# Experts of a two-layer trunk: weights as the stationary operand in plain fp32, sorted by token count

## Chip, cores and metric

One core of one Trainium2 chip. The metric is the device time of one execution in microseconds (us). The kernel before was run three times; its median is 1621.3 us (1615.85 to 1622.64).

## What is computed

A trunk of two layers over 512 tokens of 1024 features, all in fp32. Each layer mixes the tokens with four kinds of attention, adds, normalises, and then sends every token through two of sixteen experts:

```
g_sel     = argmax(x @ w_group + b_group)                  # one of 4 groups
top_logit, top_idx = top_k(expert logits of that group, 2) # 2 of its 4 experts
gate      = softmax(top_logit) * softmax(group logits)[g_sel]
for each expert e, on the rows xb of its tokens:
    h = silu(xb @ w1[e]) * (xb @ w3[e])    # 1024 -> 512
    y = h @ w2[e]                          # 512 -> 1024
x = layernorm(ALPHA * x + sum of gate * y over a token's two experts)
```

1024 assignments of tokens fall on sixteen experts a layer, unevenly. w1, w3 and w2 are 2 MB each per expert, 201 MB in all, each read once.

## The kernel before, in words

SBUF is handed out in 42 *pages* of 4 KB a partition (half a MB: one quarter of an expert's matrix) and 12 *pg* of half that; PSUM in eight *banks*. A stream (`Stream`, line 493) loads weights in the order of use on SP's queue as far ahead as free pages allow (`pump`). `conv_to` (527) turns each fp32 weight into two parts, a high one rounded to fp32r by ScalarE (`hi`) and the rest by VectorE (`lo`), in two pages, and frees the raw page. A product in near-fp32 is then three fp32r matmuls (`mm3`, 386). In attention and up to the start of the experts, strands of work are put in order by a planner (`Plan`) with a price for every operation (`cost`, 129 to 146); the experts follow in an order written out by hand (2123 to 2188).

Routing: `route` (1683) finds the two experts of each token and the counts `cnt`; `lists` (1727) works out, by comparisons and small bf16 matmuls, for each expert the token indices of its up to 128 slots (`xidx`) and their gates (`gslot`). The rows of expert 0 are gathered by matmuls with one-hot columns (`rows_0_part`, 2070: 32 matmuls in plain fp32), those of the others by an indirect DMA from DRAM (`fetch`, 1866).

An expert `e` has 128 slots. Its rows are transposed (`rows_T`, 1875, eight transposes) and split into two parts. w1 is 24 matmuls with the tokens stationary and 512 columns of weights moving (`quarter13`, 1888), into one bank; ScalarE takes the silu. w3 is the same; VectorE multiplies. The product is transposed (`hidden_T`, 1892, four transposes) and split; w2 is 24 matmuls (`quarter2`, 1904) into two banks; ScalarE multiplies by the gate (`gated`) and an indirect DMA on POOL's queue adds the rows into DRAM (`scatter`, 1915). In the hand-written order w2 of an expert comes between w1 and w3 of the next; `hidden_T` comes in the middle of that w1, `rows_T` of the next expert in the middle of w3. `use` (2049) converts three weights ahead, and `convert_ahead` (2104) converts the first six while routing runs.

Tokens beyond 128 of an expert go into extra blocks: `further_table` (1842) lists them, `further_marks` and `further_fetch` prepare the first at expert 2, and at expert 5 all engines read their number and jump (`further_blocks`, 1962). A block loads its weights by a register on SP's queue. At the end of a layer `last_rows` (2025) reads the sums back from DRAM; the last expert's rows are added by matmuls.

Attention's weighted sums are plain fp32 matmuls with 128x128 stationary and 64 moving columns: `transposed` (936) puts one transpose for each block and `accumulate` (925) one matmul for each. The router's logits (1461, and the sums at 1409) are plain fp32 matmuls with 20 moving columns.

Of the kernel before, what the change touches and what calls it, by code (L numbers as in the profile page):

```python
# [22 lines left out]
T = 512  # L23
# [23 lines left out]
LOOK_AHEAD = 3  # L47
# [12 lines left out]
CONV_AHEAD = 6  # L60
CONV_PAGES = 6
# [7 lines left out]
def trunk(ctx, tc, x, w_in, b_forget, g_cq, g_ckv, w_uq, w_ukv, g_head, w_out, ln1_g, ln1_b,  # L69
# [352 lines left out]
    thr = const.tile([128, 3], F32, name="thr")  # L422
    jx = const.tile([128, 8], F32, name="jx")
    ge48 = const.tile([128, 48], F32, name="ge48")
    e48 = const.tile([128, 48], F32, name="e48")
# [14 lines left out]
    ntab_t = const.tile([128, 8], I32, name="ntab")  # L440
    extab_t = const.tile([128, 2, 8], F32, name="extab")
    xidx_t = const.tile([128, NE], I32, name="xidx")
    gslot = const.tile([128, NE], F32, name="gslot")
    gex = const.tile([128, 7], F32, name="gex")
# [3 lines left out]
    eix_t = const.tile([128, 7], I32, name="eix")  # L448
# [11 lines left out]
    rk_t = const.tile([128, 48], F32, name="rk")  # L460

    def load_consts():
# [17 lines left out]
        nc.gpsimd.tensor_copy(thr, ci[:, 16:19])  # L480
        nc.gpsimd.tensor_copy(desc4, ci[:, 19:23])
        nc.gpsimd.tensor_copy(ge48, ci[:, 24:72])
        nc.gpsimd.tensor_copy(e48, ci[:, 72:120])
        nc.gpsimd.tensor_copy(jx, ci[:, 120:128])
# [3 lines left out]
        nc.gpsimd.tensor_copy(e_of, ci[:, 160:176])  # L488
        nc.gpsimd.tensor_copy(vals.rearrange("p c t v -> p (c t v)"), ci[:, 176:216])
# [3 lines left out]
    class Stream:  # L493
# [7 lines left out]
        def add(self, src, a, b, extra=None):  # L501
            self.items.append((src, a, b, extra))
            return len(self.items) - 1

        def emit_dma(self):
            src, a, b, extra = self.items[self.dma_i]
# [15 lines left out]
        def need(self, n):  # L522

            c = max(0, n + 1 - self.conv_i)
            return c + max(0, n + 1 - self.dma_i) + (c > 0)

        def conv_to(self, n, by_pool=False):
            n = min(n, len(self.items) - 1)
            while self.conv_i <= n:
# [3 lines left out]
                _, a, b, extra = self.items[i]  # L533
                r = self.raws.pop(i)
                h = page(list(r.shape), F32R)
# [4 lines left out]
                if by_pool:  # L540
                    nc.gpsimd.tensor_tensor(l_, r, f32(h), op=OP.subtract)
                else:
                    lo(l_, r, h)
# [10 lines left out]
    for l in range(L):  # L554
        wf = const.tile([128, 8, 4], F32, name=f"wf{l}")
        wfs.append(wf)

# [15 lines left out]
    for l in range(L):  # L573
# [6 lines left out]
        def w13(w, e, q):  # L580
            return ws.add(w[l, e, q * 256:(q + 1) * 256, :].rearrange("(k p) f -> p k f", p=128), 2, 512)

        for e in range(NE + 1):
            if e < NE:
                moe_q[l, e, "w1"] = [w13(w1, e, q) for q in range(4)]
            if e > 0:
                moe_q[l, e - 1, "w2"] = [ws.add(w2[l, e - 1, j * 128:(j + 1) * 128, :].rearrange(
                    "(o p) c -> p o c", o=1), 1, D) for j in range(4)]
            if e < NE:
                moe_q[l, e, "w3"] = [w13(w3, e, q) for q in range(4)]  # L590
# [1056 lines left out]
    for l in range(L + 1):  # L1647
# [11 lines left out]
        if l < L:  # L1659
            ws.max_raw, ws.limit = 3, 1 << 30  # L1660
# [9 lines left out]
        got_rows, fetched, gated_ = Event(), Event(), Event()  # L1670
# [12 lines left out]
        def route():  # L1683
# [41 lines left out]
            plan.spawn(lists(s1, s2), first=1)  # L1725

        def lists(s1, s2):
# [66 lines left out]
            rel(o)  # L1794
            yield Need(evs=[got_rows] + [ev["x1", t] for t in range(NT)])
            for e in range(1, ROWS):
                fetch(e, xidx[:, e:e + 1], rows[e])
# [44 lines left out]
        def further_table():  # L1842
            fl, rk_ = st(48), rk_t
            nc.vector.tensor_tensor(fl.rearrange("p (e c) -> p e c", c=3), cnt.unsqueeze(2).to_broadcast([128, NE, 3]),
                                    thr.unsqueeze(1).to_broadcast([128, NE, 3]), op=OP.is_gt)
# [421 lines left out]
```

## Time and profile before

| | |
|---|---|
| median of three runs | 1621.3 us (1615.85 to 1622.64) |
| the profiled execution | 1618.36 us, span 1616.5 us |
| mean granted TensorE clock | 0.939 |
| experts of layer 0, of layer 1 | about 457 to 765 us, 1255 to 1590 us |
| read from HBM, written | 287.81 MB, 31.00 MB |

Busy time of an engine is the time in which it has an instruction under way. A matmul is recorded with the load of its stationary operand (PEld) apart from the pass of its moving columns (PE). Durations of single PE records overlap, so the price of a record is read from the distance between starts. The granted clock is 1.00 at 2.4 GHz and 0.50 at 1.2 GHz. "idle before" with a name after an arrow is the time an engine stood still and what ended it.

### The profile page before, as it was taken

What the parts mean: (1) busy time and instruction counts of PE and PEld (TensorE: products, weight loads), DVE (VectorE), ACT (ScalarE), POOL (GpSimd) and SP (SyncE); (2) the same over time, 40 slices, a digit from 0 to 9 for tenths busy, and PEclk for the clock granted to TensorE, in tenths of its full rate; (3) what the DMA queues carried; (4) which work ended last, traced back from release to release, by engine and by line L of the source; (5) the groups of instructions that cost most, each with busy time, mean ns of one, the idle gap of its engine ahead of it and who ended that gap; (6) DMA issues with size and microseconds to landing.
All of it is one profiled execution on the core that took longest, in us unless ns stands there. A gap on an engine that the chain in (4) does not pass through costs nothing. (4 is left out here: it accounts for less than half of the span.)

```text
span 1616.5 us, 22987 instructions
## 1 busy us (share of the span) xinstructions
PE 1460.0 (90%) x8084; PEld 1246.8 (77%) x8084; DVE 1147.6 (71%) x1963; ACT 933.9 (58%) x1717; POOL 343.3 (21%) x355
## 2 busy tenths in 40 slices
PE   7999989989699899998699998989786998899994
PEld 7978878877587688886699987878665776688883
DVE  4745576475889789988774546645658996599987
ACT  5435455543367688886643534545424776588883
POOL 1511120230412122221421112002204221122212
PEclk9989999999799999999798999989887998899997
DMA  9201211264589899996330102204544998699963
GB/s 265 66 1 40 79 53 40 93 222 144 196 310 335 282 364 349 348 354 217 105 98 14 40 27 92 68 18 146 201 170 168 318 321 308 233 369 351 361 216 131
DMA packets 154238, 303.68 MB, mean 188 GB/s; under 512 B 23755, under 2 KB 47003, under 8 KB 154104
## 3 DMA queue, kind: packets, MB, share of 16 engines
q1 hardware_dynamic: 138680, 269.74, 47.3%
q0 software_dynamic: 14240, 32.20, 6.9%
q8 instruction: 68, 1.11, 0.3%
q14 instruction: 66, 0.54, 0.1%
q10 hardware_dynamic: 1184, 0.08, 0.1%
HBM read 287.81 MB, written 31.00 MB: 197 GB/s over the span
## 5 line engine op out<-in xcount | busy, mean ns | idle before, releaser
L242 PE MATMUL bank<-page,page 128*128 128x512 f32 (+5 forms) x4736 | 1022.3, 367 | 51.7 <-DVE page L242 28.6
L242 PEld LDWEIGHTS bank<-page,page 128*128 128x128 f32 (+2 forms) x4736 | 806.7, 201 | 174.5 <-DVE page L242 38.5
L242 DVE TENSOR_TENSOR page<-page,page 128x1024 fp32r<-128x1024 f32 (+3 forms) x532 | 604.4, 1178 | 154.3 <-ACT page L242 127.5
L242 ACT ACTIVATE page<-page 128x1024 fp32r<-128x1024 f32 (+3 forms) x510 | 492.4, 1024 | 36.6 <-DMA page<-in_w_in_dram 11.2
L242 PE MATMUL bank<-page,pg 128*128 128x512 f32 (+1 forms) x1568 | 309.7, 344 | 9.0 <-ACT pg L242 5.1
L242 PEld LDWEIGHTS bank<-page,pg 128*128 128x128 f32 x1568 | 262.6, 197 | 52.0 <-ACT pg L242 7.1
L242 ACT ACTIVATE page<-bank 128x256 f32<-128x256 f32 (+7 forms) x227 | 113.2, 522 | 182.5 <-PE bank L242 114.2
L242 ACT ACTIVATE pg<-bank 128x512 fp32r<-128x512 f32 (+4 forms) x209 | 97.5, 475 | 198.2 <-PE bank L242 197.9
L242 POOL DMA_INDIRECT yd<-page,xidx x30 | 47.6, 1588 | 392.9 <-ACT page L242 321.5
L242 PE MATMUL bank<-cid,pg 128*128 128x128 f32 (+1 forms) x500 | 85.6, 288 | 28.6 <-ACT pg L242 19.4
L242 POOL TENSOR_TENSOR page<-pg,pg 128x256 f32<-128x256 f32 (+1 forms) x56 | 50.6, 917 | 273.6 <-DVE pg L242 217.2
L242 POOL TENSOR_TENSOR page<-page,page 128x1024 f32<-128x1024 f32 (+5 forms) x34 | 67.7, 1999 | 152.6 <-ACT page L242 99.2
L242 PE MATMUL bank<-cid,page 128*128 128x128 f32 (+1 forms) x608 | 87.8, 282 | 13.3 <-DVE page L242 5.3
L242 DVE TENSOR_TENSOR page<-bank,page 128x512 fp32r<-128x512 f32 (+3 forms) x114 | 70.7, 646 | 34.7 <-ACT page L242 34.5
L242 PEld LDWEIGHTS bank<-cid,pg 128*128 128x128 f32 (+1 forms) x500 | 60.2, 146 | 43.3 <-ACT pg L242 25.3
L242 PEld LDWEIGHTS bank<-cid,page 128*128 128x128 f32 (+1 forms) x608 | 72.2, 144 | 23.2 <-DVE page L242 7.6
L242 ACT ACTIVATE pg<-pg 128x256 f32<-128x256 f32 (+4 forms) x132 | 59.8, 460 | 13.7 <-DVE pg L242 10.0
L242 ACT ACTIVATE page<-bank,gslot 128x512 f32<-128x512 f32 (+1 forms) x64 | 43.9, 690 | 41.2 <-PE bank L242 41.2
L242 POOL CAST page<-page 64x512 fp32r<-64x512 f32 x48 | 29.9, 623 | 137.0 <-ACT page L242 101.1
L242 POOL DMA_INDIRECT page<-x1d,xidx x30 | 45.9, 1530 | 45.1 <-DMA page<-in_w_dram 37.8
L242 DVE COPY pg<-bank 128x256 f32<-128x256 f32 (+3 forms) x73 | 35.1, 483 | 26.7 <-PE bank L242 26.6
L242 DVE SCALAR_TENSOR_TENSOR page<-bank,page 64x512 fp32r<-64x512 f32 (+1 forms) x32 | 22.0, 688 | 30.0 <-ACT page L242 29.7
(204 smaller groups left out, 977.1 us busy)
## 6 DMA issues: line engine op xcount, KB each, us to landing
page<-in_w_dram SPq DMA_DIRECT2D x396, 512.0 KB
page<-in_w_in_dram SPq DMA_DIRECT2D x64, 512.0 KB
page<-in_w_out_dram SPq DMA_DIRECT2D x16, 512.0 KB
x1d<-page SPq DMA_DIRECT2D x8, 512.0 KB
yd<-page SPq DMA_DIRECT2D x8, 512.0 KB
page<-yd SPq DMA_DIRECT2D x8, 512.0 KB
scr<-pg POOLq DMA_DIRECT2D x16, 132.0 KB, 2.0
pg<-scr POOLq DMA_DIRECT2D x16, 132.0 KB, 4.6
```

Source lines behind the costliest of these rows:

```text
L242: r = f(*args, **kw)
```

## The change

The weights of an expert are no longer converted. A raw quarter stays in its page and is the stationary operand, 128x128 at a time; the tokens are the moving operand in plain fp32. Hidden values come out with features in the partitions, so w2 needs no transposed hidden; its result does, and is transposed back to one row a slot (`slots`) before the gate, which ScalarE and VectorE share. Experts 0 to 2 keep their places; the other thirteen are put in order of their counts, on the chip (`ranks`), and the place in that order has a fixed number of slots, 66 to 128. SP reads each expert's number into a register and loads its weights by it. There may be up to twelve extra blocks in the place of seven. The scatter of an expert moves from behind its w2 to the middle of the next w3. The diff, cut to its core:

```diff
-LOOK_AHEAD = 3
+N_FIRST = 3
+SLOTS = (96, 96, 96, 128, 104, 96, 92, 88, 76, 72, 68, 66, 66, 66, 66, 66)
+N_EX = 12
...
     def conv_to(self, n):
...
+                if whole:
+                    self.parts[i] = r,
+                    self.conv_i += 1
+                    continue
...
+    def in_order(l, e):
+        if (l, e) not in places:
+            places[l, e] = nc.values_load(order_t[0:1, e:e + 1], engines=(mybir.EngineType.SP,),
+                                          min_val=0, max_val=NE - 1)
+        return places[l, e]
...
+        def expert(w, l, e, a, b, k):
+            if e < N_FIRST:
+                return w[l, e, a:b, :].rearrange("(k p) f -> p k f", k=k)
+            return lambda: w[l][bass.ds(in_order(l, e), 1), a:b, :].rearrange("a (k p) f -> p (a k) f", k=k)
...
-            ws.max_raw, ws.limit = 3, 1 << 30
+            ws.max_raw, ws.limit = 3, moe_q[l, N_FIRST - 1, "w3"][3] + 1
...
+        def ranks():
+            key, k1, own, rank = st(NE), st(NE), st(1), st(1)
+            nc.vector.scalar_tensor_tensor(key, cnt, 16.0, key_add, op0=OP.mult, op1=OP.add)
+            nc.vector.tensor_tensor(k1, key, e_off, op=OP.mult)
+            nc.vector.tensor_reduce(own, k1, axis=AX.X, op=OP.add)
+            nc.vector.tensor_scalar(k1, key, own, None, op0=OP.is_gt)
+            nc.vector.tensor_reduce(rank, k1, axis=AX.X, op=OP.add)
+            nc.vector.tensor_scalar(e_rank, eidx, rank, None, op0=OP.is_equal)
+            ranked.set()
...
+            nc.vector.tensor_copy(order_t, rf)
...
         def lists(s1, s2):
...
-            yield Need(banks=1)
+            yield Need(banks=1, evs=[ranked])
             o = bank([128, 2, NE])
             for v in range(5):
-                nc.tensor.matmul(o[:, int(v > 1)], lhsT=xs[:, v].rearrange("p a b -> p (a b)"), rhs=e_of,
+                nc.tensor.matmul(o[:, int(v > 1)], lhsT=xs[:, v].rearrange("p a b -> p (a b)"), rhs=e_rank,
...
-        def rows_T(g):
-            h = page([128, 8, 128], F32R)
-            l_ = page([128, 8, 128], F32R)
+        def rows_T(g, n):
+            h = page([128, 8, n])
             for i in range(2):
-                b = bank([128, 4, 128])
+                b = bank([128, 4, n])
                 for j in range(4):
-                    nc.tensor.transpose(b[:, j], g[:, (4 * i + j) * 128:(4 * i + j + 1) * 128], cid)
-                hi(h[:, 4 * i:4 * i + 4], b)
-                lo(l_[:, 4 * i:4 * i + 4], b, h[:, 4 * i:4 * i + 4])
+                    nc.tensor.transpose(b[:, j], g[0:n, (4 * i + j) * 128:(4 * i + j + 1) * 128], cid[0:n, 0:n])
+                copy(i, h[:, 4 * i:4 * i + 4], b)
...
-        def quarter13(o, xx, w, q):
+        def quarter13(o, x, w, q):
             for k in range(2):
-                mm3(o, [a[:, 2 * q + k] for a in xx], [p[:, k] for p in w], q == 0 and k == 0, q == 3 and k == 1)
+                for c in range(4):
+                    nc.tensor.matmul(o[:, c], lhsT=w[:, k, c * 128:(c + 1) * 128], rhs=x[:, 2 * q + k],
+                                     start=q == k == c == 0, stop=q == 3 and k == 1 and c == 3)
...
-        def quarter2(ys, ht, w, j):
-            for n in range(2):
-                mm3(ys[n], [a[:, j] for a in ht], [p[:, 0, n * 512:(n + 1) * 512] for p in w], j == 0, j == 3)
+        def quarter2(ys, h, w, j):
+            for c in range(8):
+                nc.tensor.matmul(ys[c // 4][:, c % 4], lhsT=w[:, 0, c * 128:(c + 1) * 128], rhs=h[:, j],
+                                 start=j == 0 and c % 4 == 0, stop=j == 3 and c % 4 == 3)
...
+        def slots(yt, n):
+            o = [bank([n, 4, 128]) for _ in range(2)]
+            for c in range(8):
+                nc.tensor.transpose(o[c // 4][:, c % 4], yt[:, c], cid)
...
+        def gated(yt, n, g):
+            o, held = slots(yt, n)
+            yo = page([n, D])
+            nc.scalar.activation(yo[:, 0:512], o[0], AF.Copy, scale=g[0:n])
+            nc.vector.tensor_scalar(yo[:, 512:1024], o[1], g[0:n], None, op0=OP.mult)
...
-        plan.spawn(wait_for_experts())
...
         for e in range(NE + 1):
             if e < NE:
+                n = SLOTS[e]
+                h1 = bank([128, 4, n])
+                for q in range(4):
                     i = moe_q[l, e, "w1"][q]
                     quarter13(h1, xs_[e], use(i), q)
                     used(i)
-                if q == 1 and e:
-                    ht = hidden_T(prev)
+                sl = hidden(h1, n)
             if e:
...
-                    quarter2(ys, ht, use(i), j)
+                    quarter2(ys, prev, use(i), j)
                     used(i)
-                if e < NE:
-                    scatter(gated(ys, gslot[:, e - 1:e]), xidx[:, e - 1:e])
-                if e == NE - 1:
-                    last_rows(last)
+                yt = columns(ys, n_prev)
...
+                if q == 2 and e:
+                    scatter(gated(yt, n_prev, gslot[:, e - 1:e]), n_prev, xidx[:, e - 1:e])
+                    if e == NE - 1:
+                        last_rows(last)
```

`hidden` is the silu into a pg; `columns` copies the two banks of w2 into a page, one by ScalarE and one by VectorE (`copy`). Extra blocks use the same functions with 128 slots.

## Rows read from the trace of the kernel before

**Rows 1.** The page: span and busy time of the engines.

```profile
span 1616.5 us, 22987 instructions
...
PE 1460.0 (90%) x8084; PEld 1246.8 (77%) x8084; DVE 1147.6 (71%) x1963; ACT 933.9 (58%) x1717; POOL 343.3 (21%) x355
```

**Rows 2.** Nine experts of layer 0: length, busy PE, PEld, DVE, ACT, POOL, clock, DMA share, GB/s.

```profile
572.95:590.65 17.70, 17.70 (x88) 14.74 (x86) 15.00 (x16) 14.99 (x18) 4.20 (x3) 1.00 1.04 390
...
714.63:732.36 17.73, 17.73 (x88) 14.74 (x86) 16.11 (x17) 14.90 (x18) 1.59 (x1) 1.00 0.92 322
sum 159.41, PE 159.41 PEld 132.63 DVE 143.84 ACT 134.82 POOL 34.75; mean PE 17.71 PEld 14.74 DVE 15.98 ACT 14.98 POOL 3.86
```

**Rows 3.** Timeline of TensorE, one expert of layer 0: start, length, instruction, count.

```profile
590.65 2.99 PE L242 MATMUL bank<-page,page 128*128 128x512 f32 x12
593.48 5.60 PE L242 MATMUL bank<-page,pg 128*128 128x512 f32 x24
...
601.64 1.04 PE L242 MATMUL bank<-cid,page 128*128 128x128 f32 x8
602.44 5.74 PE L242 MATMUL bank<-page,page 128*128 128x512 f32 x24
```

**Rows 4.** Timeline of TensorE, attention: transposes and weighted sums of 64 columns.

```profile
309.12 1.89 PE L242 MATMUL bank<-page,pg 128*128 128x64 f32 x16
...
357.11 0.61 PE L242 MATMUL bank<-cid,pg 128*128 128x128 f32 x4
357.56 1.00 PE L242 MATMUL bank<-page,pg 128*128 128x64 f32 x8
...
374.43 0.56 PE L242 MATMUL bank<-page,pg 128*128 128x64 f32 x4
```

**Rows 5.** Row gather (128 columns), logits (20): timeline; windows (busy PEld, clock, DMA).

```profile
420.83 3.77 PEld L242 LDWEIGHTS bank<-wg,page 128*128 128x128 f32 x32
424.43 1.44 PEld L242 LDWEIGHTS bank<-cid,page 128*128 128x128 f32 x8
...
445.40 8.77 PEld L242 LDWEIGHTS bank<-pg,page 128*128 128x128 f32 x64 [1.20 <-issue]
...
449.00:454.00 5.00, 5.00 (x47) 1.00 0.61 236
...
445.40:448.40 3.00, 3.00 (x15) 0.50 0.98 269
```

**Rows 6.** DMA issues: the experts' weights.

```profile
page<-in_w_dram SPq DMA_DIRECT2D x396, 512.0 KB
```

**Rows 7.** Timeline of TensorE: the lists of layer 0, and the marks at expert 2.

```profile
456.72 0.28 PE L242 MATMUL bank<-e_of,pg 128*128 128x16 bf16 x5 [1.58 <-DVE pg L242]
...
505.77 2.03 PE L242 MATMUL bank<-page,page 128*128 128x512 f32 x6 [0.33 <-DVE page L242]
```

**Rows 8.** Timeline of TensorE: the branch at expert 5 of layer 0.

```profile
560.57 2.25 PE L242 MATMUL bank<-page,page 128*128 128x512 f32 x6 [4.09 <-PEq L1965]
564.51 1.94 PE L242 MATMUL bank<-cid,page 128*128 128x128 f32 x8 [1.68 <-DVEq L1965]
```

**Rows 9.** Timeline of TensorE: the extra block of layer 1 and behind it.

```profile
1360.67 0.80 PE L242 MATMUL bank<-page,page 128*128 128x512 f32 x1 [5.92 <-ACT page L242]
...
1390.60 1.65 PE L242 MATMUL bank<-page,page 128*128 128x512 f32 x6 [0.45 <-PEq L1965]
...
1398.63 0.50 PE L242 MATMUL bank<-page,page 128*128 128x512 f32 x1 [1.41 <-ACT page L242]
```

**Rows 10.** Matmuls of 20 columns: timeline; windows (busy PE, clock, DMA).

```profile
82.36 1.86 PEld L242 LDWEIGHTS bank<-wg,pg 128*128 128x128 f32 x16 [0.22 <-issue]
84.14 2.21 PEld L242 LDWEIGHTS bank<-pg,pg 128*128 128x128 f32 x19
...
86.50:87.00 0.50, 0.50 (x4) 0.87 0.00 0
87.00:87.50 0.50, 0.50 (x3) 0.50 0.00 0
```

More of the change, by code (lines that the diff above doesn't have):

```diff
@@ L522, in need, with conv_to @@
         def need(self, n):
-            c = max(0, n + 1 - self.conv_i)
+            c = sum(not i[4] for i in self.items[self.conv_i:n + 1])
             return c + max(0, n + 1 - self.dma_i) + (c > 0)
-        def conv_to(self, n, by_pool=False):
+        def conv_to(self, n):
             n = min(n, len(self.items) - 1)
@@ L1794, in lists @@
             rel(o)
+            listed.set()
             yield Need(evs=[got_rows] + [ev["x1", t] for t in range(NT)])
             for e in range(1, ROWS):
-                fetch(e, xidx[:, e:e + 1], rows[e])
+                fetch(SLOTS[e], xidx[:, e:e + 1], rows[e])
         def gates():
@@ L1904, in quarter2 @@
-        def quarter2(ys, ht, w, j):
-            for n in range(2):
-                mm3(ys[n], [a[:, j] for a in ht], [p[:, 0, n * 512:(n + 1) * 512] for p in w], j == 0, j == 3)
-        def gated(ys, g):
-            yo = page([128, D])
-            for n in range(2):
-                nc.scalar.activation(yo[:, 512 * n:512 * n + 512], ys[n], AF.Copy, scale=g)
-            rel(*ys)
-            return yo
-        def scatter(yo, idx):
-            nc.gpsimd.indirect_dma_start(out=yd[l], out_offset=bass.IndirectOffsetOnAxis(ap=idx, axis=0),
+            return h
@@ new lines, in hidden, with columns @@
+        def hidden(h1, n):
+            sl = pg([128, 4, n])
+            nc.scalar.activation(sl, h1, AF.Silu)
+            rel(h1)
+            return sl
+        def columns(ys, n):
+            yt = page([128, 8, n])
+            for i in range(2):
+                copy(i, yt[:, 4 * i:4 * i + 4], ys[i])
+            rel(*ys)
+            return yt
+        def slots(yt, n):
+            o = [bank([n, 4, 128]) for _ in range(2)]
+            for c in range(8):
+                nc.tensor.transpose(o[c // 4][:, c % 4], yt[:, c], cid)
+            rel(yt)
+            return [z.rearrange("p a b -> p (a b)") for z in o], o
@@ L2149, in trunk @@
                     lo(last.x[t][1], xt[t], last.x[t][0])
-                last.y = [page([128, D], F32R) for _ in range(2)]
-                g = gslot[:, e - 1:e]
+                last.y = [page([n_prev, D], F32R) for _ in range(2)]
+                g = gslot[0:n_prev, e - 1:e]
                 for n in range(2):
@@ L2155, in trunk @@
                     lo(o[1], ys[n], o[0], g)
[L2156 removed]
+                rel(*held)
                 if l + 1 < L:
```

290 lines of the change are left out of this document (143 added, 147 removed).

## The prediction

> **What bounds the kernel now.** I began with the shares of the engines over the whole span: TensorE is busy 90% of it [rows 1]. That is a mean over attention and experts, so I went to the stage that the change rewrites. The windows cut layer 0's experts at the same point of nine successive experts [rows 2]: each is 17.7 us, TensorE busy all of it, at full granted clock, with VectorE 16.1 us and ScalarE about 15 us busy and the DMA engines at 0.92 to 1.04 of their time. Everything is nearly full, but TensorE alone never idles, so it sets the period. The timeline of one expert [rows 3] shows what fills it: 72 one-record matmuls of 512 columns (12 of them from 590.65 to 593.48, 0.236 us each; 24 of them from 593.48, some 0.23 us each), eight transposes of the rows (0.79 us from 601.64 to 602.44, 0.099 us each) and four of the hidden at the same price. 72 x 0.23 + 12 x 0.099 = 17.7.
>
> So the conversions that the change removes, VectorE's and ScalarE's, lie beside TensorE and are worth nothing in these nine windows. What the change is worth is what it does to TensorE's own work.
>
> **What a plain fp32 matmul costs here.** The kernel already has such matmuls, with 128x128 stationary and few moving columns. The weighted sums of attention follow the transposes of the same blocks one for one in the code (`transposed` and `accumulate`), and the trace has two records for each: four transposes, then eight records of 64 columns [rows 4]. The row gather of expert 0 is 32 matmuls a layer and 64 records [rows 5]. Price of a record: (1.89 - 1.00) / 8 = 0.111 us and (1.00 - 0.56) / 4 = 0.110 us at 64 columns [rows 4]; at 128 columns about 45 records in 5 us at full clock, 0.111 us (the window counts 47 with those cut at its edges) [rows 5]; at 20 columns 3.60 us from the first of 32 weight loads to the transposes behind them, 0.112 to 0.118 us [rows 5]. The price does not move between 20 and 128 columns: each record loads 128 columns of weights, and that fills its time. The planner's own price (line 136, 0.85 ns a weight column or 1.67 ns a moving column, whichever is more) would make 111 ns of one such matmul at 66 columns; the rows say 222.
>
> **The change, step by step.**
>
> The experts' matmuls. w1, w3 and w2 become 32 matmuls each, 96 an expert in the place of 72, every one with a stationary tile of its own: 192 records x 0.111 = 21.3 us, whatever the slots. Transposes: eight of the rows as before, eight back to slots in the place of four of the hidden: 16 x 0.099 = 1.6 us (the fewer columns may make them cheaper by some tenths; taken at nothing). The new period is 22.9 us against 17.7: +5.2 us an expert, 32 experts, **+166 us**. The slots of 66 to 128 buy TensorE nothing by these rows. Bounds for the record: 0.107 (below all rows) to 0.115 us, which over 6144 records is 25 us either way.
>
> The Trainium skill, in "TensorE: Matmul & The Clock Gate", section "Back-to-back issue gap", gives about 81 ns for each load-and-matmul pair in a sustained stream at 128 columns. By it the expert would take an estimated 192 x 0.081 + 1.6 = 17.1 us and the change would cost nothing; the 111 ns of the rows here disagree, and the sum above keeps to the rows.
>
> The conversions, hidden transposes' evictions and the second page of every weight. They go: no instruction of them was on TensorE's path in the windows [rows 2], so 0 there. The new copies, the half-and-half gating and the silu of fewer columns are shorter than what goes, and each has at least 3 us of matmuls between it and its reader.
>
> The DMA. At 0.92 to 1.04 of 17.7 us it has some 17.5 us of work an expert [rows 2]; 17.5 is below 22.9, so it falls behind TensorE as the second limit and prefetch gets deeper, a weight taking one page in the place of two. Sorted experts need a register load and a dynamic source on SP's queue: 13 loads of a register a layer, among 396 weight loads in all [rows 6]. SP waits for the order table, with all the later weight loads queued behind that wait, but 32 loads in fixed order (experts 0 to 2, some 60 us of TensorE) stand before it. Cost 0; if that cover failed, the loads of expert 3 would start late once, a few us a layer. On POOL the scatter moves from behind w2 into the middle of w3 and so behind the fetch of the rows two experts on; the fetch is then earlier, the scatter later, and only expert 14's has a reader that matters (the end of the layer, below).
>
> Ranks. Fifteen small VectorE operations a layer, six of them ahead of the five matmuls of the lists, which get a wait for the ranks, already wait 1.58 us for VectorE [rows 7], and have all of expert 0 queued behind them on TensorE. The conversions and splits that sat between them on VectorE go. Taken at 0, bounds -1.5 to +1.5 us a layer.
>
> The marks of the extra block at expert 2. TensorE waited there for conversions that were late: 0.33 us idle, and six matmuls in 2.03 us where six take 1.4 [rows 3, 7]. With none left I take -1 us a layer, -2 in all (0 to -5).
>
> The branch at expert 5. TensorE stands 4.09 us in the jump and then runs cold and waits for VectorE [rows 8]; the jump stays, the wait for a conversion goes: -3 us for both layers (0 to -5).
>
> Extra blocks. The reference's routing of these inputs puts at most 87 tokens on an expert of layer 0, and 142 and 97 on the largest two of layer 1: with 128 and 104 slots by rank there is still one extra block in all, as now (396 loads = 2 x 192 + 12 [rows 6]). It took TensorE from 1360.67 to 1390.60, 30 us, most of it waiting for conversions and cold [rows 9]. After: 21.3 + 1.6 us of matmuls, some 3 us at half clock after the jump, and 3 to 5 us for its first loads and its own evictions, again about 30: 0, bounds -5 to +8. Behind it TensorE waited 1.41 us and more for a weight to be converted [rows 9]: -3 us (0 to -5).
>
> The end of a layer. The last expert loses the hidden's transposes and their evictions and gains the copy to columns and the slots' transposes; the reading back of the sums starts later, behind expert 14's scatter in the middle of w3. 0, an estimate, bounds -4 to +6 for both layers.
>
> Sum: 166 - 2 - 3 - 3 = **+158 us**. The profiled execution took 1618.4 us by the clock for a span of 1616.5; the median of the three runs is 1621.3, 0.2% more. 1618 + 158 = **1776 us**.
>
> **The rivals.**
>
> *The clock falls under narrow matmuls.* TensorE's granted clock fell to 0.50 near 86.9 us behind 35 records of 20 columns, while TensorE had no idle time at all [rows 10]. The new experts, of 66 to 128 columns, lie between those 20 and the 128 of the row gather, behind which the clock rose (0.50 until 448.4, 1.00 from 449.0 [rows 5]). For it: the first row. Against it: the second; of 64 columns the trace has only bursts. Price: a half-clock record is 3.00 us / 14 = 0.214 us [rows 5], so an expert at half clock costs 192 x 0.103 = 20 us more. Five experts a layer have 66 slots: ten at half clock give 1776 + 198 = 1974 us, half of that if it alternates, about 1875.
>
> *The weight load hides in a long stream (not slower).* The rows of 64 and 20 columns are bursts of 4 to 35 records. If in a stream of 32 matmuls a record went below (17.7 + 0.3 - 1.6) / 192 = 0.085 us (the 0.3 being the 8 us of stalls saved, over 32 experts), the change would not be slower, and DMA would bound it near 17 us an expert: 32 x 0.6 + 8 = 27 us less, some 1590 us. Against it: the 64 records of 128 columns are one stream and still took 0.111 us each. The page named above would put the price there.
>
> *Not what it says.* If the ranks let an expert outgrow its slots, an extra block more would run, some 30 to 38 us each: 1810. By the same routing at least four slots stay free on every expert except the one of 142 tokens, and that one has the single block.
>
> **How the numbers follow.** The sum at 0.111 us a record gets 0.79, the falling clock 0.13, the hidden load 0.06, more blocks 0.02. The first case's own range, by its bounds, is 1735 to 1815. The 80% range is carried up to 1880 to take in an alternating clock; full half clock and the hidden load stay out. A measurement of this kernel can tell about 0.5% (8 us) from no change. Faster by more comes only from the hidden load, 0.06; within it 0.02; slower 0.92.
>
> **What would show it.** Right: two records a matmul in the experts, 0.111 us each from expert 3 (128 slots) down to expert 15 (66), a period of 22.9 us with TensorE never idle at clock 1.0, VectorE and ScalarE well under half busy, DMA near 0.75. Wrong: a period that shrinks with the slots (then moving columns set the price), a granted clock of 0.5 in the last experts of a layer, or TensorE waiting for weights.

## The result, and the profile after

The changed kernel takes 1759.9 us (median of four runs, 1757.8 to 1766.4), the kernel before 1621.2 us beside it: 1.087 times as long, interval 1.083 to 1.091. The prediction was 1776 us with a range of 1735 to 1880. The profiled execution took 1757.8 us, 139.4 us more than that of before. Of the repeated executions below one, of b_no_ahead, took 2099.9 us at a mean granted clock of 0.638; its ratio leaves it out.

The page of the changed kernel, span and busy time, answers to [rows 1]:

```profile
span 1756.0 us, 30585 instructions
PE 1619.0 (92%) x12176; PEld 1513.5 (86%) x12176; DVE 696.6 (40%) x1590; ACT 503.7 (29%) x1250; POOL 327.5 (19%) x367
```

VectorE went from 71% to 40% and ScalarE from 58% to 29%: the conversions are gone. TensorE has half as many records again. Two windows of one expert's length in layer 0, from w3 of the seventh place to w3 of the eighth and from w3 of the fourteenth to w3 of the fifteenth (columns as in [rows 2]):

```profile
604.81:627.70 22.89, 22.89 (x210) 22.89 (x209) 2.37 (x4) 2.09 (x4) 3.48 (x3) 1.00 0.94 321
764.33:787.09 22.76, 22.76 (x211) 22.76 (x210) 2.04 (x4) 1.85 (x4) 1.52 (x1) 1.00 0.20 58
```

A period of 22.8 us against 17.7 [rows 2], TensorE and its weight loads busy all of it, VectorE and ScalarE at 2 us, the clock at 1.00 with 66 slots too. In the last window the DMA engines have little left to load. The timeline of TensorE, w2 of the expert with 128 slots and of one with 66:

```profile
544.58 7.33 PE L242 MATMUL bank<-pg,page 128*128 128x128 f32 x64
551.75 3.72 PE L242 MATMUL bank<-page,page 128*128 128x104 f32 x32
...
757.18 7.31 PE L242 MATMUL bank<-pg,page 128*128 128x66 f32 x64
764.33 0.94 PE L242 MATMUL bank<-page,page 128*128 128x66 f32 x7
```

From start to start, 64 records of 128 columns take 551.75 - 544.58 = 7.17 us, 64 of 66 columns 764.33 - 757.18 = 7.15 us: 0.112 us each, whatever the columns.

TensorE in the routing, at the branch of expert 5 and at the end of layer 0 answers to [rows 5, 7, 8]:

```profile
439.42 0.20 PE L242 MATMUL bank<-asb,tri 128*128 128x16 bf16 x1 [7.98 <-DVE asb L242]
...
451.92 0.28 PE L242 MATMUL bank<-e_rank,pg 128*128 128x16 bf16 x5 [1.20 <-DVE pg L242]
452.05 10.94 PE L242 MATMUL bank<-page,page 128*128 128x96 f32 x96
...
579.05 3.70 PE L242 MATMUL bank<-page,page 128*128 128x96 f32 x16 [2.42 <-PEq L2052]
...
818.57 7.36 PE L242 MATMUL bank<-pg,page 128*128 128x66 f32 x64 [0.59 <-DVE pg L242]
...
832.79 0.79 PE L242 MATMUL bank<-page,pg 128*128 128x512 f32 x1 [5.70 <-ACT page L242]
```

The wait in the jump is 2.42 us in the place of 4.09, and VectorE no longer holds TensorE behind it. The first expert starts at 452.05 us, 4.8 earlier than before. At the end of the layer stands a new wait of 5.70 us: ScalarE, and through it TensorE, wait for the sums to be read back from DRAM.

Cutting both traces at the same instructions says where the 139.4 us are. The experts are cut from the first matmul of expert 0 to the end of the last w3, the end of a layer from there to the first matmul by the identity (`cid`, 128x512). In layer 0 these are 456.86, 747.14 and 764.82 us before, 452.05, 817.98 and 845.59 us after. "All the rest" is the time of the profiled execution less the other rows:

| stretch | before, us | after, us | difference |
|---|---|---|---|
| experts, layer 0 | 290.3 | 365.9 | +75.6 |
| experts, layer 1 | 322.5 | 389.0 | +66.5 |
| ends of the two layers | 34.6 | 50.0 | +15.4 |
| all the rest (attention, routing) | 971.0 | 952.9 | -18.1 |

### The profile page after: what moved, and what is told of

The parts are those of the page before. It is cut to its first block, busy times and chain, and to the rows that moved or that the text cites. A ratio compares the mean times of both kernels' runs of the same rounds, so it can differ in the third digit from the quotient of the medians.

```text
span 1756.0 us, 30585 instructions
## 1 busy us (share of the span) xinstructions
PE 1619.0 (92%) x12176; PEld 1513.5 (86%) x12176; DVE 696.6 (40%) x1590; ACT 503.7 (29%) x1250; POOL 327.5 (19%) x367
## 5 line engine op out<-in xcount | busy, mean ns | idle before, releaser
L242 PE MATMUL bank<-page,page 128*128 128x256 f32 (+13 forms) x7376 | 1116.1, 307 | 41.0 <-DVE page L242 23.6
L242 PEld LDWEIGHTS bank<-page,page 128*128 128x128 f32 (+1 forms) x7376 | 991.3, 198 | 97.9 <-DVE page L242 28.7
L242 PE MATMUL bank<-pg,page 128*128 128x96 f32 (+8 forms) x2240 | 260.1, 278 | 4.3 <-DVE pg L242 4.3
L242 PEld LDWEIGHTS bank<-pg,page 128*128 128x128 f32 x2240 | 256.8, 194 | 4.9 <-DVE pg L242 2.5
L242 ACT ACTIVATE page<-bank 128x256 f32<-128x256 f32 (+14 forms) x228 | 107.8, 482 | 512.6 <-PE bank L242 445.6
L242 DVE TENSOR_TENSOR page<-page,page 128x1024 fp32r<-128x1024 f32 (+6 forms) x138 | 140.6, 1037 | 83.0 <-ACT page L242 70.1
L242 PE MATMUL bank<-page,pg 128*128 128x64 f32 (+2 forms) x776 | 125.0, 296 | 17.7 <-ACT page L242 9.7
L242 PEld LDWEIGHTS bank<-page,pg 128*128 128x128 f32 (+1 forms) x776 | 112.8, 204 | 30.4 <-ACT page L242 11.4
L242 PE MATMUL bank<-cid,page 128*128 128x128 f32 (+16 forms) x872 | 115.4, 272 | 10.8 <-DVE page L242 5.5
L242 ACT ACTIVATE page<-page 128x1024 fp32r<-128x1024 f32 (+4 forms) x114 | 102.7, 925 | 23.9 <-DMA page<-in_w_in_dram 10.7
```

What stands on the lines that cost most here:

```text
L242: r = f(*args, **kw)
```

## The experiments

Twelve kernels ran; each was timed beside the kernel before on its chip, which took 1614 to 1619 us.

**a_ladder: fewer columns.** From the seventh place on, the slots go from 66 to 128 down to 64 to 20; the tokens beyond them are left out.

```diff
-SLOTS = (96, 96, 96, 128, 104, 96, 92, 88, 76, 72, 68, 66, 66, 66, 66, 66)
+PLACES = (96, 96, 96, 128, 104, 96, 92, 88, 76, 72, 68, 66, 66, 66, 66, 66)
+SLOTS = (96, 96, 96, 128, 104, 96, 64, 64, 48, 48, 32, 32, 20, 20, 20, 20)
...
```

`PLACES` takes the place of `SLOTS` in the table of extra blocks, so that no block is added.

> The changed kernel with 64, 64, 48, 48, 32, 32, 20, 20, 20, 20 slots from place 6 on (tokens beyond them are left out). If the load of 128 weight columns sets the price, a record stays at 0.111 to 0.112 us down to 20 columns and an expert at 22.3 to 22.8 us. If moving columns had a part in it, the narrow experts get shorter, by up to 11 us each at 20 columns (16 or more experts, total 1650 or less). If the granted clock falls under narrow matmuls, it falls to 0.50 at 20 columns at the latest, where rows of before saw it fall, and each such expert takes about 44 us: with the last four of each layer about 1757 + 8 x 21 = 1925 us. I expect the last, with the step from 1.00 to 0.50 somewhere between 66 and 20.

Measured 2100.3 us. Windows of layer 0 (columns as in [rows 2]), then TensorE's timeline:

```profile
624.00:640.00 16.00, 16.00 (x148) 15.88 (x146) 1.53 (x3) 1.78 (x4) 0.00 (x0) 1.00 0.95 334
640.00:646.00 6.00, 6.00 (x47) 6.00 (x46) 0.42 (x1) 0.00 (x0) 3.37 (x3) 0.81 0.71 214
```

```profile
615.41 9.04 PE L243 MATMUL bank<-page,page 128*128 128x64 f32 x80
624.29 7.31 PE L243 MATMUL bank<-pg,page 128*128 128x64 f32 x64
...
640.83 2.40 PE L243 MATMUL bank<-page,page 128*128 128x48 f32 x20
...
677.29 17.14 PE L243 MATMUL bank<-page,page 128*128 128x48 f32 x80
694.23 6.17 PE L243 MATMUL bank<-pg,page 128*128 128x48 f32 x28
```

80 records of 64 columns take 8.88 us at full clock (0.111), 80 of 48 columns 16.94 us at half clock (0.212). The price is flat at either level. Through both experts with 64 slots the clock stayed at 1.00. It fell at about 643.7 us (a mean of 0.81 in the 6 us from 640 is 1.00 for 3.7 us and 0.50 behind), in w1 of the first expert with 48 slots, while TensorE was busy in all of every window, and stayed at 0.50 to the last w3 of the layer. I had priced that only for the last four places, so my time was too low. In the changed kernel five experts of 66 slots in a row kept 1.00. The first rival of the prediction was thus two steps of the ladder away.

**a_onepass: one record a matmul.** Weights and tokens are rounded once to fp32r (the low parts are left out), with TensorE's order kept. The conversions come back, one a weight, three weights ahead of TensorE.

```diff
                 if whole:
-                    self.parts[i] = r,
+                    h = page(list(r.shape), F32R)
+                    if i % 2:
+                        nc.vector.tensor_copy(h, r)
+                    else:
+                        hi(h, r)
+                    rel(r)
+                    self.parts[i] = h,
...
```

> The changed kernel with weights and tokens rounded to fp32r in one part (the low parts are left out), by ScalarE and VectorE in turn, stationary and moving as in the change: one record a matmul. If two records a matmul are the cause, TensorE needs 96 x 0.11 + 1.6 = 12 us an expert and the DMA engines set the period, 16.5 to 17.5 us: 1757 - 32 x 5.5 = about 1580 us, with DMA near 1.0. If the kind of a matmul doesn't matter, nothing changes (1757 us).

Measured 1757.3 us, the time of the changed kernel with half its records. TensorE's timeline at 128 and at 66 slots, and two windows:

```profile
542.36 3.75 PE L242 MATMUL bank<-pg,page 128*128 128x128 f32 x32
545.95 1.94 PE L242 MATMUL bank<-page,page 128*128 128x104 f32 x16
...
722.76 7.01 PE L242 MATMUL bank<-pg,page 128*128 128x66 f32 x32
729.58 3.60 PE L242 MATMUL bank<-page,page 128*128 128x66 f32 x16
```

```profile
540.00:560.00 20.00, 20.00 (x163) 20.00 (x162) 8.77 (x14) 11.77 (x15) 6.25 (x4) 0.87 0.94 268
...
720.00:740.00 20.00, 20.00 (x100) 19.76 (x100) 3.70 (x7) 7.24 (x10) 2.78 (x3) 0.50 0.70 232
```

32 records at 128 slots take 3.59 us, again 0.112 each; at 66 slots 6.82 us, 0.213 each, at a clock of 0.50. So the price belongs to a record with 128 stationary columns, in fp32r as in plain fp32, and what halving their number saved, the clock took back. The clock had been at 0.50 in the first experts too, from a wait of 3.32 us for a conversion at about 456 us on, and was back at 1.00 by 535 us. At 555.0 us it fell again, in records of 96 and then 104 columns, with TensorE busy all the time, and stayed at 0.50 to the last w3 (22.95 us an expert at 66 slots). The miss of 177 us is in the main this clock, which I had taken as held; TensorE also waited for conversions here and there.

**a_half: half the stationary columns.** Every stationary tile is cut into two of 64 columns, with the same result and twice the matmuls, in the order left half, right half, left half.

```diff
                 for c in range(4):
-                    nc.tensor.matmul(o[:, c], lhsT=w[:, k, c * 128:(c + 1) * 128], rhs=x[:, 2 * q + k],
+                    for p in (0, 64):
+                        nc.tensor.matmul(o[p:p + 64, c], lhsT=w[:, k, c * 128 + p:c * 128 + p + 64], rhs=x[:, 2 * q + k],
...
```

> The changed kernel with every stationary tile of 128 columns cut into two of 64, so twice the matmuls, the same result. If a record costs the load of its stationary columns or the pass of its moving columns, whichever is longer, then half the columns load in 0.055 us and the period follows the slots: 384 records x 0.058 = 22 us at 66 slots, 31 us at 96, 42 us at 128; about 1967 us in all. If a record had a fixed price of 0.111 us, every expert takes 44 us: about 2440 us.

Measured 1658.1 us: 100 us less than the changed kernel, where I had expected at least 200 more. TensorE's timeline, records of 128 and of 96 columns, and the group of 66 columns (busy time, mean ns, idle before it):

```profile
509.28 7.21 PE L242 MATMUL bank<-page,page 128*64 128x128 f32 x128
516.32 5.45 PE L242 MATMUL bank<-pg,page 128*64 128x96 f32 x128
521.70 1.09 PE L242 MATMUL bank<-cid,page 128*128 128x128 f32 x8
```

```profile
L242 PE MATMUL bank<-page,page 128*64 128x66 f32 x2560 | 85.2, 224 | 16.4 <-issue 15.4 <-DMA page<-in_w_dram 1.0
```

128 records of 128 columns take 7.04 us (0.055 each), 128 of 96 columns 5.38 us (0.042). Now the price does follow the moving columns: what had hidden them was the 128-column load. Narrow records then meet a new limit, idle time that the trace puts down to "issue" (85.2 us busy and 16.4 us idle in this group). I didn't test its cause. Two readings of the 0.055 were left, and the next two kernels tell them apart.

**a_half_grouped: the same records in another order.** All left halves of a quarter first, then all right halves.

```diff
-                for c in range(4):
-                    for p in (0, 64):
+                for p in (0, 64):
+                    for c in range(4):
...
```

> The tiles cut into two of 64 columns as in a_half, same matmuls and same result, only the order differs: all matmuls of one half of the output columns (four for w1 and w3, eight for w2), then all of the other half, in the place of alternating. Two readings of a_half's 0.0345 us (66 columns) to 0.055 us (128 columns) a record are left. Reading A: a record's pass takes one moving column per 2.4 GHz cycle and a 64-column load hides behind it; the order is then indifferent: 1658 us within 10, records as in a_half. Reading B: in plain fp32 a record's pass takes two cycles a column, and the two halves of the array work side by side, so that neighbours in alternating order overlap and neighbours in the same half don't: about 0.107 us a record at 128 columns, 0.08 at 96, 0.055 to 0.06 at 66; with about 80 slots on the mean an expert is 384 x 0.068 + 1.6 = 27.7 us in the place of 22.8 of the changed kernel, about 1757 + 32 x 4.9 = 1914 us.

Measured 1736.7 us. TensorE's timeline, records of 128 columns in runs of eight (w1, w3) and of sixteen (w2) in the same half:

```profile
518.14 8.16 PE L242 MATMUL bank<-page,page 128*64 128x128 f32 x125
526.03 0.30 PE L242 MATMUL bank<-pg,page 128*64 128x96 f32 x1
...
553.54 10.93 PE L242 MATMUL bank<-pg,page 128*64 128x128 f32 x123
564.21 0.30 PE L242 MATMUL bank<-page,page 128*64 128x104 f32 x1
```

7.89 / 125 = 0.063 us a record in runs of eight, 10.67 / 123 = 0.087 in runs of sixteen, 0.055 when they alternate. Order matters, and more so the longer the runs: reading A falls. Reading B gets the direction, but its 1914 us were far too high: it priced a record of 128 columns in the same half at 0.107 us, and 0.063 and 0.087 were measured. I take it that records of the two halves still overlap where the runs meet; no run shows that by itself.

**a_moving: the roles turned back.** Raw fp32 weights move, 512 columns at a time, and the tokens' 66 to 128 columns are stationary. The hidden is transposed, the result is not, and the scatter is again right behind w2. All else of the change stays.

```diff
-                for c in range(4):
-                    nc.tensor.matmul(o[:, c], lhsT=w[:, k, c * 128:(c + 1) * 128], rhs=x[:, 2 * q + k],
-                                     start=q == k == c == 0, stop=q == 3 and k == 1 and c == 3)
+                nc.tensor.matmul(o, lhsT=x[:, 2 * q + k], rhs=w[:, k], start=q == k == 0, stop=q == 3 and k == 1)
...
```

> The raw weights, the sorted order, the slots and all of routing stay; only the roles are turned back: the tokens' columns (66 to 128) are stationary and 512 columns of raw weights move, in plain fp32; the hidden is transposed (four transposes) and the result is not (eight fewer). An expert is 24 matmuls, 48 records. Reading A (one column a cycle, 512 / 2.4 GHz = 0.213 us): 48 x 0.22 + 1.2 = 11.8 us, below what the weights' transfers take, some 16.5 us an expert: about 1757 - 32 x 6.2 = 1560 us, faster than both. Reading B (two cycles a column, 0.427 us a record): 48 x 0.427 + 1.2 = 21.7 us, about 1757 - 32 x 1.1 = 1720 us, still slower than before.

Measured 1698.7 us: reading B. TensorE's timeline, w2 of one expert and what follows it, and the next w2:

```profile
690.24 7.03 PE L242 MATMUL bank<-page,pg 128*68 128x512 f32 x16
697.11 3.60 PE L242 MATMUL bank<-page,page 128*66 128x512 f32 x8
...
711.59 7.03 PE L242 MATMUL bank<-page,pg 128*66 128x512 f32 x16
```

16 records in 697.11 - 690.24 = 6.87 us: 0.429 us for 512 columns, against 0.23 for a record in the kernel before [rows 3], which multiplies parts rounded to fp32r. At 2.4 GHz 512 columns at two cycles each are 0.427 us. A plain fp32 matmul is two such records, four cycles a column, where the three records of before are three. Hence the same 24 matmuls an expert take 20.6 us raw and 16.6 us in three parts, and the period is 711.59 - 690.24 = 21.35 us. The period is some 1.45 us shorter than the changed kernel's 22.8, 46 of the 59 us over 32 experts; the rest lies mainly at the ends of the layers, where the scatter is earlier and w2's result needs no transposing (in layer 1 13.0 us from the last w2's start to the matmul by the identity, in the place of 21.8).

Worked out from a_moving's 0.429 us for 512 columns, a pass of 128 columns takes an estimated 0.107 us, and in a_half records of 128 columns in alternating halves came every 0.055 us: two passes ran beside each other. The Trainium skill, "TensorE: Matmul & The Clock Gate", section "The mechanism" (under the packing of small matmuls), says that tiles of the array can hold different weights and compute different slices of the output, so that their matmuls overlap. The 0.055 us agree with it.

**a_fixed128: no sorting.** Fixed order and 128 slots everywhere.

```diff
-N_FIRST = 3
-SLOTS = (96, 96, 96, 128, 104, 96, 92, 88, 76, 72, 68, 66, 66, 66, 66, 66)
+N_FIRST = 16
+SLOTS = (128,) * 16
```

> The changed kernel with its experts in fixed order and 128 slots each (no ranks used for order, no numbers read into registers). By the flat price of a record, 0.111 us at any number of columns up to 128, only transposes, copies and DMA rows grow: 0.2 to 0.4 us an expert, 1760 to 1768 us. If the slots by rank bought TensorE time, it would be well above: by columns (66 to 128, 83 on the mean of the sixteen places) 192 x 0.111 x (128 / 83 - 1) = 11 us an expert, 2100 us.

Measured 1763.7 us. Its timeline:

```profile
616.86 7.31 PE L242 MATMUL bank<-pg,page 128*128 128x128 f32 x64
624.00 3.74 PE L242 MATMUL bank<-page,page 128*128 128x128 f32 x32
```

64 records in 7.14 us, as with 66 slots. The period is 640.04 - 616.86 = 23.2 us in the place of 22.8 to 22.9, by the larger transposes. The time lies among the changed kernel's own four (1757.8 to 1766.4): what sorting and slots by rank are worth is too little for one run to tell, and TensorE's records got nothing from them.

**a_scatter: the end of a layer.** The scatter of expert 14 comes behind the first quarter of the last w3 instead of the third.

```diff
-                if q == 2 and e:
+                if q == (0 if e == NE - 1 else 2) and e:
```

> The changed kernel with expert 14's gate and scatter behind the first quarter of expert 15's w3 in the place of the third, 3.6 us earlier. If the end of the layer waits for the sums read back from DRAM, the 5.7 us of layer 0 and some 3 us of layer 1 that TensorE stands there shrink by up to 3.6 us each: 4 to 7 us less, about 1752 us. If the wait is for ScalarE's own queue, nothing.

Measured 1753.1 us in one run. Its trace, at the place of the 5.70 us above:

```profile
820.62 7.36 PE L242 MATMUL bank<-pg,page 128*128 128x66 f32 x64 [0.59 <-DVE pg L242]
...
831.75 0.50 PE L242 MATMUL bank<-page,pg 128*128 128x512 f32 x1 [2.62 <-ACT page L242]
```

From the last w2's start to the matmul by the identity (844.36 us here, 845.59 in the changed kernel) it is 23.7 us in the place of 27.0, and in layer 1 18.3 in the place of 21.8. The later scatter thus costs some 3.4 us a layer.

**b_no_ahead and b_no_pool: the 18 us outside the experts.** Both are the kernel before; one loses the strand that converts six weights ahead, in the other that strand's subtractions never go to POOL.

```diff
-        plan.spawn(wait_for_experts())
```

> The kernel before, without the strand that converts the first six expert weights while routing runs (no conversions on ScalarE, VectorE and POOL until the experts start). My theory of the 18 us that the change gained outside the experts: a quarter of it or more a layer comes from this strand standing in the way of the last normalisation and of the router. It predicts the row gather some 4 us earlier in each layer. The same weights are then converted inside expert 0, three ahead of TensorE, where ScalarE and VectorE were nearly full: that gives back 0 to 10 us a layer. Net 1610 to 1630. The rival (the strand lay beside other work and the 18 us come from elsewhere) predicts the row gather where it was, 445 us, and a time of 1621 to 1640.

```diff
-                    ws.conv_to(i, by_pool=plan.clock["POOL"] + 1200.0 < plan.clock["DVE"])
+                    ws.conv_to(i)
```

> The kernel before, with the early conversions' subtractions on VectorE alone and never on POOL. If the 4.13 us that VectorE's sums of 160 elements take just before routing come from POOL's subtraction running beside it, they fall to about 1 us; VectorE has 1.2 us more of its own for each subtraction. Row gather 1 to 3 us earlier a layer, 1615 to 1620 us. If POOL is not the cause, 4.13 us stay and the time is 1621 to 1626.

b_no_ahead: 1622.5 us, 1.0024 times before (0.9999 to 1.0049), no change. b_no_pool: 1636.1 us, 1.0103 (1.0075 to 1.0132), above both expectations. VectorE and TensorE in layer 0's routing, first of before (with POOL's subtraction among its four operations), then of b_no_ahead, then of b_no_pool:

```profile
431.98 6.64 POOL L242 TENSOR_TENSOR page<-page,page 128x384 f32<-128x384 f32 x4 [2.23 <-ACT page L242]
435.58 4.13 DVE L242 TENSOR_TENSOR page<-page,page 128x160 f32<-128x160 f32 x2
443.76 0.20 PE L242 MATMUL bank<-asb,tri 128*128 128x16 bf16 x1 [12.30 <-DVE asb L242]
```

```profile
437.76 0.85 DVE L242 TENSOR_TENSOR page<-page,page 128x160 f32<-128x160 f32 x1
441.65 0.20 PE L242 MATMUL bank<-asb,tri 128*128 128x16 bf16 x1 [7.97 <-DVE asb L242]
```

```profile
439.44 1.98 DVE L242 TENSOR_TENSOR page<-page,page 128x160 f32<-128x160 f32 x2
445.48 0.20 PE L242 MATMUL bank<-asb,tri 128*128 128x16 bf16 x1 [10.15 <-DVE asb L242]
```

Without the strand TensorE's wait for the router falls from 12.30 to 7.97 us, the changed kernel's 7.98; layer 1 shows the same (12.29 and 7.99). The strand did stand in the way of the router. The row gather of layer 0 is only 2.1 us earlier (443.33 us), because the logits before it came 2.2 us later in this execution. From layer 0's end to layer 1's row gather it is 470.5 us in the place of 478.7 (in the changed kernel 466.0), but of these 8.2 us only the 4.3 of the router's wait are the strand's: its first conversion in layer 1 starts at 1229.9 us, behind all of attention, and the rest is a clock that fell near 871 us in the trace of before and not in this one (below). Without the strand the kernel gives back what it gains: from the first expert's start to the layer's end it takes 4.2 and 7.5 us longer, as expert 0 waits for its conversions. b_no_pool confirms half: with POOL's subtraction gone the two sums take 1.98 us in the place of 4.13, but VectorE then does the subtractions itself, 1.21 us each, before and behind the router, and the row gather is 3 us later.

**a_paired: two halves at once.** If two narrow passes go side by side, a stationary of 64 tokens leaves half the array free. This kernel is a_moving with 64 slots in the last seven places, where w1 goes to columns 0 to 63 and w3 to 64 to 127, and likewise the two halves of w2's result.

```diff
+                for q in range(4):
+                    for k in range(2):
+                        for o, v in ((o1[0:n], wa), (o3[64:64 + n], wb)):
+                            nc.tensor.matmul(o, lhsT=xs_[e][:, 2 * q + k], rhs=v[:, k], start=q == k == 0, stop=q == 3 and k == 1)
...
```

> a_moving (raw weights moving, tokens stationary) with one more change: the last seven places of a layer have 64 slots, which by the routing of these inputs hold all their tokens, and their matmuls go in pairs, one to each half of the output columns: w1 to columns 0 to 63 and w3 to 64 to 127 with the same stationary tokens, and likewise the two halves of w2's result (the last expert's w2 excepted). If the two halves of the array work side by side, a paired record costs 0.43 / 2 = 0.215 us and an expert of 64 slots 48 x 0.215 + 1.1 = 11.4 us in the place of 21.3: 14 x 9.9 = 139 us less, and 7 us back for the two last w2: 1698.7 - 132 = 1567 us, faster than before by 3%. The weights' transfers (some 16.5 us an expert) then bind in part: nine places at 21.3 let them run ahead, so up to 30 us may come back, 1567 to 1597. Rival: neighbours in the two halves overlap only in short records, as in a_half, where a load of 64 columns was hidden and no pass was; then the paired experts stay at 21 us and the time at 1690 to 1710.

Measured 1609.9 us, 0.9926 times before (0.9898 to 0.9955): faster than the kernel before by 0.7%, clear of noise but small. TensorE's timeline, one paired expert, then the end of the layer:

```profile
658.61 5.37 PE L243 MATMUL bank<-page,page 128*64 128x512 f32 x24
...
666.81 3.65 PE L243 MATMUL bank<-page,pg 128*64 128x512 f32 x16
670.29 5.32 PE L243 MATMUL bank<-page,page 128*64 128x512 f32 x24
...
718.70 1.08 PE L243 MATMUL bank<-page,pg 128*64 128x512 f32 x4 [0.49 <-DMA page<-in_w_dram]
...
754.27 0.79 PE L243 MATMUL bank<-page,pg 128*128 128x512 f32 x1 [5.25 <-ACT page L243]
```

16 records in 3.48 us, 0.218 each, half of a_moving's 0.429, and 11.7 us from one such expert to the next: the mechanism holds in full. The time is 13 us over the expected range, because the gain runs out at the end of a layer. TensorE waits for weights one by one in the last two experts, then 5.25 us for the sums, and at the matmul by the identity its clock is at 0.50. What each of these costs was not measured apart.

**a_paired_end and a_mixed** try to get that back: an earlier scatter in the last place, and besides, paired places put between wide ones. The line below is a_mixed against a_paired_end.

```diff
-SLOTS = (96, 96, 96, 128, 104, 96, 92, 88, 76) + (64,) * 7
+SLOTS = (96, 96, 96, 128, 64, 104, 64, 96, 64, 92, 64, 88, 64, 76, 64, 64)
...
```

> a_paired with the w2 of the fourteenth expert one quarter of w1 and w3 earlier in the last place, so that its scatter, and the reading back of the sums behind it, start some 2 to 3 us earlier. In a_paired TensorE waited 5.25 us for ScalarE at that point of layer 0 and its clock was at 0.50 behind it. If the scatter is what was late: 2 to 3 us a layer, and up to 5 more where the clock then holds: 1595 to 1606 us beside a_paired's 1609.9. If the weights' transfers are what is late there (they land one by one in the last two experts), the wait stays and the time is 1608 to 1611.

> a_paired_end with the places interleaved, places of 64 slots (11.6 us of TensorE) between the wide ones (21.3 us), in the place of all seven at the end. The mean is then 17.1 us an expert and the weights need some 16.5, so that they keep pace: the waits for weights in the last two experts (in a_paired's layer 0 from 717 to 740 us, 14.4 us an expert on the mean of the seven in the place of 11.6 and the one plain w2) go, 10 to 15 us a layer: 1572 to 1590 us, 2 to 3% faster than before. Rival: the transfers bind in every place as a whole (some 16.5 us an expert whatever the order), and the sum stays: 1597 to 1608 us.

a_paired_end: 1606.6 us, 0.9941 (0.9912 to 0.9970), not to be told from a_paired; the wait shrank to 1.83 us, and layer 0's experts with their end became 2.9 us shorter, layer 1's 0.7 us longer. a_mixed: 1655.8 us, 1.0254 (1.0223 to 1.0285), a clear miss of both its expectation and its rival. Its TensorE:

```profile
622.35 1.46 PE L244 MATMUL bank<-cid,page 92*128 92x92 f32 x8 [6.18 <-DMA page<-x1d,xidx]
...
702.15 1.25 PE L244 MATMUL bank<-cid,page 76*128 76x76 f32 x8 [8.74 <-DMA page<-x1d,xidx]
```

The waits for weights in the last experts did go. In their place TensorE waits for the rows of the next expert, here 6.2 and 8.7 us: a wide place asks for them near its end, behind a scatter on POOL's queue, and the paired place behind it wants them half-way through, 5 to 9 us later, while the transfers by the index table take 8.1 to 16.2 us to land. An earlier fetch was not tried.

## Why the prediction was right

*The bound, and the price of a record.* Both held. TensorE alone sets the experts' period; 0.111 us a record was predicted and 0.112 measured, at any number of slots, and a period of 22.9 was measured as 22.8. The reason given, a load of 128 columns that fills the record's time, is what a_ladder (20 to 64 columns), a_fixed128 (128) and a_onepass (one record a matmul) bear out, and a_half by its opposite: with 64 columns to load the price falls. What I had not seen is that at 128 moving columns the pass itself is an estimated 0.107 us (from a_moving), so that both limits meet there. The Trainium skill, "TensorE: Matmul & The Clock Gate", section "LDWEIGHTS (loading the stationary operand)", puts a load at its columns divided by 1.2 ns, 107 ns for 128, and the flat 0.111 us agree. The 81 ns of the Trainium skill's section "Back-to-back issue gap", which the prediction set beside the rows, were reached in no stream of these experts with 128 stationary columns.

*The conversions.* "Worth nothing" is right for the nine windows it was read from and wrong as a rule for the kernel. This is the step that failed: the prediction looked at that wait in the experts alone and put the stretches outside them at 0. The strand that converts ahead also runs during routing, and there VectorE is on TensorE's path. Of the 18 us gained outside the experts, b_no_ahead shows 8.6 to be this strand, 4.3 in each routing. Another 4.8 us are the clock, in layer 1's attention, where no conversion of an expert runs. Before (first two lines) and after (last two), from the records of 20 columns to the same twelve matmuls:

```profile
869.60 1.91 PE L242 MATMUL bank<-wg,pg 128*128 128x20 f32 x16
883.58 3.00 PE L242 MATMUL bank<-page,page 128*128 128x512 f32 x12
...
948.13 1.91 PE L242 MATMUL bank<-wg,pg 128*128 128x20 f32 x16
957.35 2.99 PE L242 MATMUL bank<-page,page 128*128 128x512 f32 x12
```

That is 13.98 us with the clock at 0.50 from 872 us on, and 9.22 at 1.00; in b_no_ahead, which kept its clock too, 9.20. At or just behind these records of layer 1 the clock fell in ten of the fourteen traces, variants of the changed kernel among them, and held in four. That the change held it is therefore not shown; it may be luck of the profiled executions. The remaining 4.7 us, 1.1 of them between the row gather and the first expert, I could not place.

*Marks, branch and extra block.* The experts up to the last w3 cost +142 us. The prediction's own terms make 154: 166 less some 4 for the two last w2, which the table counts with the ends, less 8. Half of the miss of 12 is the extra block. Layer 1's experts took 32.2 us longer than layer 0's before, 23.0 after, so the block became 9.2 us cheaper, where I had 0 and 3 us behind it. The 23.0 us are as much as its own matmuls (192 x 0.111 + 1.6 = 22.9): what it waits besides, as 3.95 us in the jump against 2.42 in layer 0, is made up elsewhere. The marks at expert 2 give some 3 us more: from w2 to w2 that expert was 3.0 us over its neighbours in each layer before and 0.6 after, where I had 1 us a layer. Some 2 us are the transposes, cheaper with fewer slots (a period of 22.76 us with 66), which I had taken at nothing. The branch saved 1.4 us in layer 0, as forecast.

*End of a layer.* Forecast at 0 (-4 to +6); measured +15.4, some 4 of it the dearer w2, so +11, outside the bounds. I had named the mechanism, the scatter of expert 14 behind the middle of w3, and undersized it; a_scatter shortens the two ends by 6.7 us. The other 4 are not placed. That error and the 12 us too many for the experts nearly cancel, which is luck: it leaves the 18 us outside the experts as the distance between forecast and measurement.

*DMA, ranks.* As forecast: TensorE waits for no weight in the experts of either layer, the DMA engines are at 0.76 over them, and the wait before the lists is 1.20 us against 1.58.

*The rivals.* The clock held at 66 slots; a_ladder shows it holding with 64 and falling with 48. The hidden load did not come. There was no additional block: 396 weights were loaded, as before. The chances have a slip: a case of more blocks, at 1810 us, is slower too, so "slower" should have had 0.94.

## What to carry to other kernels

Price a stream of matmuls by the larger of two things read from the trace, the load of the stationary columns and the pass of the moving ones. Here a plain fp32 matmul is two records of two cycles a moving column, each with its own load, so with 128 stationary columns a moving operand of fewer than 128 columns buys nothing, and three rounded passes of 512 columns beat it. A wait that is "hidden" in one stage has to be looked up in every stage where the same work runs, and a stationary of 64 columns is worth pairing with another (0.218 us a record in the place of 0.429).

## What the runs showed of the hardware

- A record with 128 stationary columns cost 0.111 to 0.112 us at full clock with 64, 66 and 128 moving columns, and 0.21 us at half clock with 20 to 48.
- Twice as many matmuls were faster: two half-width records, 0.055 us apart, ran beside each other where one full-width record takes 0.111. In runs of eight and of sixteen in the same half they came every 0.063 and 0.087 us.
- TensorE's clock fell to 0.50 in stretches with no idle time at all: in a_ladder at 48 plain fp32 columns, in a_onepass at 96 to 104 fp32r columns. It stayed at 1.00 at 64 plain fp32 columns for two experts and at 66 for five.
- Two sums of 160 columns on VectorE took 4.13 us beside operations on POOL that included a subtraction (before) and 1.98 us where POOL had one operation fewer (b_no_pool).
